# A hybrid decoder block: order of the first weight tile, a cast in two halves, and the spread of the row scale

## Chip, cores and metric

The kernel runs on one core of a Trainium2 chip. The metric is the device time of one execution in microseconds (us), as a median over runs; lower is better.

## What is computed

One decoder layer on 512 tokens of 1024 channels, all in float32. Cut to what matters here:

```python
h = rms_norm(x, g_mix_pre)                  # x * rsqrt(mean(x^2) + eps) * g
z = h @ w_in                                # 1024 x 4608: u_pool | u_rx | u_rg | two gates
xc = causal_dwconv(u_rx, conv_w, conv_b)    # 4 taps along the tokens, 1024 channels
gates = einsum('bshi,ghij->gbshj', xc by 16 heads of 64, w_gates) + b_gates
r, i = sigmoid(gates[0]), sigmoid(gates[1])
log_a = -8 * r * softplus(-lru_lambda)
h_t = exp(log_a) * h_{t-1} + sqrt(-expm1(2 log_a)) * i * xc
y_rnn = (h * gelu(u_rg)) @ w_rg_out
# pooling mixer, gated merge, w_o; then a convolutional FFN and a gated embedding: untouched here
```

## The kernel before

**Arithmetic.** Every large product is made from float32 numbers split in two parts of the type that the trace names fp32r: `hi` is the value cast (on ACT, ScalarE), `lo` is the rest (a subtraction on DVE, VectorE). A product is then three matmuls, hi·hi, hi·lo and lo·hi (`mm3`, L220 to L224). The weight is the loaded operand, the 512 tokens stream past it, so a full matmul is 128 x 128 weights against 512 columns.

**Weights.** `prep(key)` (L450 to L492) issues the transfer of a weight tile into `raw` (on SP's queue), the cast `hi` (ACT, L480; the first tile by pieces, L477) and the subtraction `lo` (DVE, L191 by `sub`). There are six buffers each for raw, hi and lo; the cast of a tile six places later in the list therefore waits until PE (TensorE) has finished with the buffer that it overwrites. `weight(key, ahead)` starts the tiles that come next.

**First stage.** x comes transposed in eight tiles; `ht(k)` is the k-th tile times the gain (hi on ACT L561, lo on DVE L562). The first four channel tiles of u_rx are computed with k outermost (L585 to L591): for each of the eight k, three products times four banks, 96 matmuls. One weight tile, key `("rx", j)`, holds 512 columns for k = 2j and 512 for k = 2j + 1. The scale rsqrt(mean(x²)) of each token is not yet known then; it goes in afterwards, when the banks are read. It is computed as a column per token tile (`rstd1`, 128 x 4, POOL), made into four diagonal matrices (`diag`, DVE L596), and spread over all partitions by four float32 matmuls against a matrix of ones (`spread_rstd`, PE L642), which stand inside the first ordinary channel tile, after its third k. ACT copies the bank to `rb` (L643).

**The recurrent branch's first half.** `in_tile(n)` (L646) is then one channel tile of z at a time, 24 matmuls. Tile by tile around them go: `evac` (DVE L656, times rb, frees the bank), `conv_first` (ACT L674), `conv_rest` (three steps on DVE L680, then the ACT cast L685 of the result), `conv_low` (DVE L689), and, from the sixth tile on, after every second one, `gates` for two channel tiles (PE L700, 12 matmuls with half the rows, six for each tile, alternating between the two banks that each tile has), the eight sigmoids that read these banks (ACT L166) and `gated` (DVE L712). A bank of `gates` is free again when its two sigmoids have read it. In between, DVE computes `decay_columns` (L617 to L636), the softplus of lru_lambda: some twenty operations on tiles of 128 x 8 named `sp`, each needing the one before, with an exponential and a logarithm on ACT; the logarithm needs another function table (ACT_TABLE_LOAD).

**PSUM.** Eight banks rotate. `gates((4, 5))` gives channel tile 5 two banks that `gates((2, 3))` used before it: the second bank of channel tile 2 and the first of channel tile 3. Likewise the first bank of channel tile 1 in `gates((0, 1))` becomes the second bank of channel tile 3 in `gates((2, 3))`.

**Order.** PE's order is the order of the program text. On ACT and DVE a scheduler places the instructions by readiness and priority; `urgent()` and `tc.high_priority` raise it, `behind(a, b)` puts a behind b on the same engine. Each engine then works through its list in that order and waits at the head of it.

Of the kernel before, what the change touches and what calls it, by code (L numbers as in the profile page):

```python
# [9 lines left out]
F32 = mybir.dt.float32  # L10
F32R = mybir.dt.float32r
AF = mybir.ActivationFunctionType
ALU = mybir.AluOpType

P = 128
S = 512
D = 1024
KD = D // P
DFF = 3 * D
NJ = DFF // P  # L20
NT = S // P
# [62 lines left out]
def block_kernel(  # L84
# [21 lines left out]
    ACT, V, PE = nc.scalar, nc.vector, nc.tensor  # L106

    const = ctx.enter_context(tc.tile_pool(name="const", bufs=1))
# [11 lines left out]
    def urgent():  # L120
        return tc.high_priority(offset=URGENT)
# [3 lines left out]
    def nm(s):  # L125
        uid[0] += 1
        return f"{s}{uid[0]}"

    def bank():
        return psum.tile([P, S], F32, tag="ps", name=nm("ps"))  # L130

    def temp(dt=F32, n=S):
        return tmp.tile([P, n], dt, tag="t", name=nm("t"))

    def slot(dt=F32):
        return mid.tile([P, S], dt, tag="m", name=nm("m"))
# [10 lines left out]
    def parts_of(n):  # L147

        return [wpool.tile([P, D], F32R, tag=t, name=nm(t))[:, :n] for t in ("hi", "lo")]

    def tiny(n=1, dt=F32):
        return small.tile([P, n], dt, tag="s", name=nm("s"))

    def behind(ins, name):
        tc.add_manual_dep(
            ins.ins,
            name,
            mybir.DependencyInfo(mybir.DependencyClass.NoSync, mybir.DependencyReason.DATA),
            reason="order on the engine",
        )  # L160
# [29 lines left out]
    def sub(o, a, b):  # L190
        return V.tensor_tensor(o, a, b, ALU.subtract)  # L191
# [7 lines left out]
    def turns(a):  # L199

        return a.rearrange("p (a b) -> p b a", a=2)
# [28 lines left out]
    ident = const.tile([P, P], F32, tag="ident", name="ident")  # L230
    make_identity(nc, ident)
    ones = slot()[:, :P]
# [122 lines left out]
        for kp in range(4):  # L355
            plan(("wpg", kp, h), rows2(w_ple_gate, kp, h))

    ready, low_of, copy_of = {}, {}, {}
    nxt = [0]


# [25 lines left out]
    def up_form(p, f):  # L387

        b = blocks
        if p == 0:  # L390
            t = block(0, f)
        elif p in UP_SUMS:
            t = block(p, {1: 11, 2: 21, 3: 22}.get(f, f))
        elif f == 1:
            for k in (11, 12, 22, 21):
                b[p, k] = block(p, k)
            b[p, 0] = wpool.tile([P, 2, S], F32, tag="sum", name=nm("sum"), bufs=1)
            t = b[p, 11]
        elif f == 6:
            add(b[p, 0], b[p, 11], b[p, 12])  # L400
            t = b[p, 11]
            add(t, b[p, 0], b[p, 22])
        elif f == 7:
            t = b[p, 12]
            add(t, t, b[p, 22])
        elif f == 4:
            t = b[p, 21]
            add(t, b[p, 11], t)
        else:
            t = b[p, {2: 21, 3: 22, 5: 0}[f]]  # L410
        if p == 0 and f != PLAIN[0]:
            late.append((f, t))
            return
        hi, lo = (v.rearrange("p (j c) -> p j c", j=2) for v in parts_of(D))
        if (p, f) in ((1, 1), (1, 5), (1, 7)):
            ins = ACT.copy(hi, t)
            if f != 1:
                behind(ins, h2_done[0])
            later[f] = hi, lo, t
            ready["up", p, f] = (hi, lo)  # L420
            return
        split(hi, lo, t)
        if p == 1 and f != 1:
            behind(last_copy[0], h2_done[0])
        if (p, f) == (1, 4):
            behind(last_sub[0], hid_done[0])
        if p > 2 and f == 6:
            behind(last_copy[0], z_done[0])
        if p > 1 and f == 3:
            behind(last_copy[0], z6_done[p])  # L430
        if p > 1 and f == 7:
            behind(last_copy[0], z_done[0])
        ready["up", p, f] = (hi, lo)
# [16 lines left out]
    def prep(key):  # L450
        if key[0] == "up" and key not in parts:
            up_form(*key[1:])
            return
        if key in parts:
            hi, lo = parts_of(D)
            for i, v in enumerate((hi, lo)):
                nc.sync.dma_start(v.bitcast(F32), parts[key][i])
            if key[0] == "up":
                hi, lo = (v.rearrange("p (j c) -> p j c", j=2) for v in (hi, lo))
            ready[key] = (hi, lo)  # L460
            return
        ap = src[key]
        n = 1
        for d in ap.shape[1:]:
            n *= d
        raw = wpool.tile([P, n], F32, tag="raw", name=nm("raw"), bufs=6)
        dst = raw if len(ap.shape) == 2 else raw.rearrange("p (k c) -> p k c", k=ap.shape[1])
        if key == order[0]:
            nc.sync.dma_start(xraw[0], x_t[0])
            for a, b in FIRST:  # L470
                nc.sync.dma_start(raw[:, a:b], ap.rearrange("p k c -> p (k c)")[:, a:b])
        else:
            nc.sync.dma_start(dst, ap)
        hi, lo = parts_of(n)
        if key == order[0]:
            for a, b in FIRST:
                ACT.copy(hi[:, a:b], raw[:, a:b])  # L477
                sub(lo[:, a:b], raw[:, a:b], hi[:, a:b].bitcast(F32))
        else:
            ins = ACT.copy(hi, raw)  # L480
            last = ins.ins.name
            if key[0] == "wpg" and key[2] == 1:
                behind(ins, last_copy[0].ins.name)
            with tc.high_priority(offset=2 * URGENT if key[0] == "wpg" and key[2] == 0 else 300 if key[0] == "in" and key[1] >= 12 else 0):
                ins = sub(lo, raw, hi.bitcast(F32))
                low_of[key] = ins.ins.name
                copy_of[key] = last
            if key[0] == "wpg" and key[2] == 1:
                behind(ins, last_low[0])
        if key[0] == "rg":  # L490
            hi, lo = (v.rearrange("p (j c) -> p j c", j=2) for v in (hi, lo))
        ready[key] = (hi, lo)  # L492

    def weight(key, ahead=AHEAD):
        i = order.index(key)
        while nxt[0] <= min(i + ahead, len(order) - 1):
            prep(order[nxt[0]])
            nxt[0] += 1
        return ready[key]
# [38 lines left out]
    def ht(k):  # L538
        return hth[k // 4][:, k % 4, :], htl[k // 4][:, k % 4, :]
# [3 lines left out]
    ht_done = []  # L543

    def load_tokens(a):
        xt = quad("C", F32)
        nc.sync.dma_start(
            xt.rearrange("p (a h) c -> p a (h c)", a=2),
            x[2 * a * P : 2 * (a + 1) * P, :].rearrange("(a p) c -> p a c", p=P),
        )  # L550
        xtok.append(xt)

    for k in range(KD):
        raw = xraw[k]
        if k == 0:
            weight(("rx", 0), ahead=0)
        else:
            nc.sync.dma_start(raw, x_t[k])
        hi, lo = ht(k)
        g = gmix[:, k : k + 1]  # L560
        ht_done.append(ACT.activation(hi, raw, AF.Identity, scale=g).ins.name)  # L561
        V.scalar_tensor_tensor(lo, raw, g, hi.bitcast(F32), ALU.mult, ALU.subtract)  # L562
        if k == 3:
            nc.sync.dma_start(col, cols)
        if k % 2 == 1 and k < 7:
            weight(("rx", k // 2 + 1), ahead=0)
        if k in (5, 7):
            load_tokens(k // 2 - 2)
# [4 lines left out]
    for a in range(2):  # L573
        xt = xtok[a]
        for b in range(2):
            v = xt[:, 2 * b : 2 * b + 2, :]
            t = 2 * a + b
# [3 lines left out]
    rstd1 = rsqrt(v4, NT)  # L581
    last_sum[0] = last_pow[0]
    sum_in_dram(chain_of(sums_of("rg"), sums_of("wo"), sums_of("up")), None)
    rx = [bank() for _ in range(4)]
    for k in range(KD):  # L585
        w = weight(("rx", k // 2), ahead=3)
        (wh, wl), (hh, hl) = w, ht(k)
        for i, (a, b) in enumerate(((wh, hh), (wl, hh), (wh, hl))):
            for m in range(4):
                o = (k % 2) * S + m * P  # L590
                PE.matmul(rx[m], a[:, o : o + P], turns(b), start=k == 0 and i == 0, stop=k == KD - 1 and i == 2)  # L591


    diag = temp()
    for t in range(NT):
        behind(V.tensor_scalar(diag[:, t * P : (t + 1) * P], ident, rstd1[:, t : t + 1], None, ALU.mult), low_of["in", 0])  # L596

    bd = quad("C").rearrange("p (s a) c -> p s (a c)", s=2)
    raw = wpool.tile([P, D], F32, tag="raw", name=nm("raw"), bufs=6)
# [38 lines left out]
    def spread_rstd():  # L638
        with urgent():
            ps = bank()  # L640
            for t in range(NT):
                PE.matmul(ps[:, t * P : (t + 1) * P], ones, diag[:, t * P : (t + 1) * P], start=True, stop=True)  # L642
            ina(ACT.copy(rb, ps))  # L643


# [350 lines left out]
    for p in range(2):  # L996
# [8 lines left out]
        if p == 0:  # L1005
            pled = dram.tile([S, D], F32, name="pled")
            pq = []
            for k in range(2):
                raw = temp()
# [232 lines left out]
    d = {}  # L1242
# [212 lines left out]
    for h in range(2):  # L1455
        for t in range(NT):
            i = 2 * (t % 2) + h
            o = temp()
            v = ple[t // 2][:, i, :]
            ins = V.scalar_tensor_tensor(v, v, rp[t], gp[:, h, :], ALU.mult, ALU.mult)  # L1460
# [3 lines left out]
            for a, b in parts:  # L1464
                ps = bank()
# [90 lines left out]
```

## Time and profile before

| what | us |
|---|---|
| three runs | 700.49, 699.56, 700.41 |
| median | 700.41 |
| the profiled execution | 699.78 |
| its span, first to last instruction | 698.0 |
| PE busy in it | 692.4 |
| DVE, ACT, POOL busy in it | 591.4, 453.9, 97.1 |
| granted TensorE clock, mean (1 is full) | 0.998 |

The span is what the instructions cover; 1.8 us of the execution lie outside it. Times inside a trace count from the start of the span. In rows of the timeline the first number is the start in us, the second the time to the end of the group, "x4" the number of instructions in it, and the bracket how long the engine was idle before it and what ended the idle time. PEld is PE's loading of weights, which overlaps its matmuls; a row with a "q" behind the engine's name is its sequencer issuing a transfer. The end of a matmul is modelled, so the pace of PE is read from start to start.

### The profile page before, as it was taken

The page shows a single profiled execution, that of the slowest core. Times are in us where ns is not written, and L with a number is a line of the kernel's source. Part 1 is how long each engine was busy: PE and PEld are TensorE (multiplying, and loading weights), DVE is VectorE, ACT ScalarE, POOL GpSimd, SP SyncE. Part 2 cuts the span into 40 slices and gives each one's busy share as a digit, 9 for nine tenths or more (in the row PEclk, how much of TensorE's full clock was granted, in tenths as well). Part 3 has the DMA queues.
Part 4 walks back from the last instruction along what each step waited for, and adds up shares of the span by engine and source line. Part 5 has one row for each costly group of instructions (what it writes and reads, how often), then busy time and mean ns, then how long its engine had stood idle before and what let it go on. Part 6 is the DMA issues. An engine that isn't in the chain of part 4 may idle for free.

```text
span 698.0 us, 11598 instructions
## 1 busy us (share of the span) xinstructions
PE 692.4 (99%) x4423; PEld 638.1 (91%) x4423; DVE 591.4 (85%) x772; ACT 453.9 (65%) x693; POOL 97.1 (14%) x123
## 2 busy tenths in 40 slices
PE   9999999999999999999999999999999999999997
PEld 8888888888888998899999999999999888888886
DVE  5698735999759998888999999999999989889962
ACT  5857789934447565489966666776667747665631
POOL 0311231321100000112011211210210310001100
PEclk9999999999999999999999999999999999999999
DMA  8999999999998897956387896897799799968011
GB/s 318 408 310 258 251 246 245 264 229 288 261 335 293 301 386 255 346 211 208 115 312 229 191 271 205 202 260 243 173 215 384 241 299 329 343 211 283 29 61 61
DMA packets 67287, 175.71 MB, mean 252 GB/s; under 512 B 6048, under 2 KB 6688, under 8 KB 66848
## 3 DMA queue, kind: packets, MB, share of 16 engines
q1 hardware_dynamic: 49808, 124.64, 49.9%
q0 software_dynamic: 17280, 50.34, 31.0%
q8 instruction: 35, 0.57, 0.3%
q14 instruction: 20, 0.16, 0.1%
q10 hardware_dynamic: 144, 0.00, 0.0%
HBM read 162.37 MB, written 62.91 MB: 323 GB/s over the span
## 4 chain that ended last, share of the span: by engine, by line
PE 99%; DVE 0%; ACT 0%; issue 0%
PE ps L222 31%; PE ps L223 31%; PE ps L224 31%; PE ps L591 3%; PE ps L1034 1%; PE ps L700 1%; PE ps L241 1%; PE ps L642 0%; ACT t L166 0%; DVE t L1474 0%; DVE t L1475 0%; PE ps L1160 0%; DVE m L233 0%; DVE mhalf L235 0%
## 5 line engine op out<-in xcount | busy, mean ns | idle before, releaser
L191 DVE TENSOR_TENSOR lo<-raw,hi 128x1024 fp32r<-128x1024 f32 (+2 forms) x199 | 230.3, 1183 | 46.1 <-ACT hi L480 29.6
L222 PE MATMUL ps<-A,hi 128*128 128x256 f32 (+1 forms) x672 | 211.9, 315 | 0.0
L224 PE MATMUL ps<-A,lo 128*128 128x256 f32 (+1 forms) x672 | 211.4, 315 | 0.0
L223 PE MATMUL ps<-A,hi 128*128 128x256 f32 (+1 forms) x672 | 211.4, 315 | 0.0
L480 ACT CAST hi<-raw 128x1024 fp32r<-128x1024 f32 (+1 forms) x118 | 118.1, 1012 | 56.7 <-PE ps L224 21.5
L222 PEld LDWEIGHTS ps<-A,hi 128*128 128x128 f32 x672 | 128.2, 191 | 8.0 <-issue 1.0
L224 PEld LDWEIGHTS ps<-A,lo 128*128 128x128 f32 x672 | 128.3, 191 | 6.9
L223 PEld LDWEIGHTS ps<-A,hi 128*128 128x128 f32 x672 | 128.3, 191 | 6.8
L222 PE MATMUL ps<-C,hi 128*128 128x256 f32 x376 | 103.4, 275 | 0.0
L223 PE MATMUL ps<-C,hi 128*128 128x256 f32 x376 | 103.2, 275 | 0.0
L224 PE MATMUL ps<-C,lo 128*128 128x256 f32 x376 | 103.2, 274 | 0.0
L195 ACT CAST hi<-raw 128x1024 fp32r<-128x1024 f32 x75 | 77.8, 1051 | 20.5 <-PE ps L223 12.8
L222 PE MATMUL ps<-hi,A 128*128 128x512 f32 x224 | 85.2, 380 | 0.0
L223 PE MATMUL ps<-lo,A 128*128 128x512 f32 x224 | 84.9, 379 | 0.0
L224 PE MATMUL ps<-hi,A 128*128 128x512 f32 x224 | 84.9, 379 | 0.0
L222 PEld LDWEIGHTS ps<-C,hi 128*128 128x128 f32 x376 | 71.8, 191 | 0.2
L223 PEld LDWEIGHTS ps<-C,hi 128*128 128x128 f32 x376 | 71.8, 191 | 0.1
L224 PEld LDWEIGHTS ps<-C,lo 128*128 128x128 f32 x376 | 71.8, 191 | 0.0
L511 POOL TENSOR_TENSOR s<-s,mhalf 128x1 f32<-128x1 f32 (+1 forms) x21 | 17.4, 829 | 262.6 <-DVE s L528 240.0
L307 POOL DMA_DIRECT2D wdsum<-in_w_down_dram x36 | 33.1, 1055 | 141.3 <-ACT t L1170 62.8
L224 PEld LDWEIGHTS ps<-hi,A 128*128 128x128 f32 x224 | 42.3, 189 | 6.0
L223 PEld LDWEIGHTS ps<-lo,A 128*128 128x128 f32 x224 | 42.4, 189 | 5.9
(206 smaller groups left out, 1072.4 us busy)
## 6 DMA issues: line engine op xcount, KB each, us to landing
raw<-in_w_up_dram SPq DMA_DIRECT2D x46, 512.0 KB, 5.9
wdsum<-in_w_down_dram POOLq DMA_DIRECT2D x36, 512.0 KB, 7.6
raw<-in_w_in_dram SPq DMA_DIRECT2D x32, 512.0 KB, 8.0
raw<-wdsum SPq DMA_DIRECT2D x24, 512.0 KB, 8.2
raw<-in_w_down_dram SPq DMA_DIRECT2D x18, 512.0 KB, 7.3
wosum<-in_w_o_dram POOLq DMA_DIRECT2D x12, 512.0 KB, 8.7
wdsum<-wdsum POOLq DMA_DIRECT2D x12, 512.0 KB, 6.6
raw<-wosum SPq DMA_DIRECT2D x8, 512.0 KB, 6.1
```

Source lines behind the costliest of these rows:

```text
L191: return V.tensor_tensor(o, a, b, ALU.subtract)
L195: last_copy[0] = ACT.copy(hi, src)
L222: PE.matmul(o, ah, bh, start=start, stop=False, **kw)
L223: PE.matmul(o, ah, bl, start=False, stop=False, **kw)
L224: PE.matmul(o, al, bh, start=False, stop=stop, **kw)
L241: PE.matmul(wps[:, :P], ones, ones, start=True, stop=True)
L307: ins = nc.gpsimd.dma_start(o, i, **kw)
L480: ins = ACT.copy(hi, raw)
L511: last_pow[0] = nc.gpsimd.tensor_tensor(y, v, mhalf[:, :n], ALU.pow).ins.name
L591: PE.matmul(rx[m], a[:, o : o + P], turns(b), start=k == 0 and i == 0, stop=k == KD - 1 and i == 2)
L700: PE.matmul(ps, bd[pr, a, o], turns(b[pr]), start=i == 0, stop=i == 2)
L1034: PE.transpose(ps[:, q * P : (q + 1) * P], a[:, q * P : (q + 1) * P], ident)
```

## The change

1. The first weight tile (k = 0): PE does all three products for banks 0 and 1, then all three for banks 2 and 3, so that the first six matmuls touch only the first 256 weight columns. For every even k the order of the products becomes (weight hi, x hi), (weight hi, x lo), (weight lo, x hi); before, and still for odd k, the weight's lo comes second.
2. The second weight tile, `("rx", 1)`: its cast and its subtraction are made in two halves of 512 columns. The first half's cast is put behind `ht(2)`'s operation on ACT, the second's behind `ht(3)`'s.
3. The spread: the four scales of a row are split in hi and lo (two 128 x 4 operations), each is multiplied with the identity into one 128 x 512 tile of type fp32r, and two fp32r matmuls of 512 columns against ones cast to fp32r replace the four float32 ones. The two diagonal operations have raised priority.

```diff
--- before.py
+++ after.py
@@ -355,7 +355,7 @@
         for kp in range(4):
             plan(("wpg", kp, h), rows2(w_ple_gate, kp, h))
 
-    ready, low_of, copy_of = {}, {}, {}
+    ready, low_of, copy_of, second = {}, {}, {}, []
     nxt = [0]
 
 
@@ -476,6 +476,10 @@
             for a, b in FIRST:
                 ACT.copy(hi[:, a:b], raw[:, a:b])
                 sub(lo[:, a:b], raw[:, a:b], hi[:, a:b].bitcast(F32))
+        elif key == ("rx", 1):
+            for a, b in (0, S), (S, 2 * S):
+                second.append(ACT.copy(hi[:, a:b], raw[:, a:b]))
+                sub(lo[:, a:b], raw[:, a:b], hi[:, a:b].bitcast(F32))
         else:
             ins = ACT.copy(hi, raw)
             last = ins.ins.name
@@ -559,6 +563,8 @@
         hi, lo = ht(k)
         g = gmix[:, k : k + 1]
         ht_done.append(ACT.activation(hi, raw, AF.Identity, scale=g).ins.name)
+        if k in (2, 3):
+            behind(second[k - 2], ht_done[-1])
         V.scalar_tensor_tensor(lo, raw, g, hi.bitcast(F32), ALU.mult, ALU.subtract)
         if k == 3:
             nc.sync.dma_start(col, cols)
@@ -585,15 +591,31 @@
     for k in range(KD):
         w = weight(("rx", k // 2), ahead=3)
         (wh, wl), (hh, hl) = w, ht(k)
-        for i, (a, b) in enumerate(((wh, hh), (wl, hh), (wh, hl))):
-            for m in range(4):
-                o = (k % 2) * S + m * P
-                PE.matmul(rx[m], a[:, o : o + P], turns(b), start=k == 0 and i == 0, stop=k == KD - 1 and i == 2)
-
-
-    diag = temp()
-    for t in range(NT):
-        behind(V.tensor_scalar(diag[:, t * P : (t + 1) * P], ident, rstd1[:, t : t + 1], None, ALU.mult), low_of["in", 0])
+        three = ((wh, hh), (wl, hh), (wh, hl)) if k % 2 else ((wh, hh), (wh, hl), (wl, hh))
+        for ms in (range(4),) if k else (range(2), range(2, 4)):
+            for i, (a, b) in enumerate(three):
+                for m in ms:
+                    o = (k % 2) * S + m * P
+                    PE.matmul(rx[m], a[:, o : o + P], turns(b), start=k == 0 and i == 0, stop=k == KD - 1 and i == 2)
+
+
+    ones_r = const.tile([P, P], F32R, tag="ones", name="ones")
+    ACT.copy(ones_r, ones)
+    rh, rl = tiny(NT, F32R), tiny(NT)
+    V.tensor_copy(rh, rstd1)
+    sub(rl, rstd1, rh.bitcast(F32))
+    diag = []
+    for r in (rh.bitcast(F32), rl):
+        d = temp(F32R)
+        with urgent():
+            ins = V.tensor_tensor(
+                d.rearrange("p (t c) -> p t c", t=NT),
+                ident[:, None, :].to_broadcast([P, NT, P]),
+                r[:, :, None].to_broadcast([P, NT, P]),
+                ALU.mult,
+            )
+        behind(ins, low_of["in", 0])
+        diag.append(d)
 
     bd = quad("C").rearrange("p (s a) c -> p s (a c)", s=2)
     raw = wpool.tile([P, D], F32, tag="raw", name=nm("raw"), bufs=6)
@@ -638,8 +660,8 @@
     def spread_rstd():
         with urgent():
             ps = bank()
-            for t in range(NT):
-                PE.matmul(ps[:, t * P : (t + 1) * P], ones, diag[:, t * P : (t + 1) * P], start=True, stop=True)
+            for i, d in enumerate(diag):
+                PE.matmul(ps, ones_r, d, start=i == 0, stop=i == 1)
             ina(ACT.copy(rb, ps))
```

The instructions move at three places. First ACT, at the start: `hi_167` is the cast of tile ("rx", 1), `A` the results of `ht`. Before:

```order
L561 ACTIVATE A_135<-m_140,gmix 128x512
L480 CAST hi_167<-raw_165 128x1024
L561 ACTIVATE A_135<-m_141,gmix 128x512
L561 ACTIVATE A_135<-m_142,gmix 128x512
L480 CAST hi_180<-raw_178 128x1024
L561 ACTIVATE A_136<-m_143,gmix 128x512
```

and with the change:

```order
L565 ACTIVATE A_135<-m_140,gmix 128x512
L565 ACTIVATE A_135<-m_141,gmix 128x512
L481 CAST hi_167<-raw_165 128x512
L565 ACTIVATE A_135<-m_142,gmix 128x512
L481 CAST hi_167<-raw_165 128x512
L484 CAST hi_182<-raw_180 128x1024
```

The cast of ("rx", 1), one instruction ahead of two `ht` operations before, is now two, one behind each of them.

Second ACT, around the logarithm of `decay_columns`: `sp` are its 128 x 8 tiles, `hi` casts of coming weight tiles, `m` and `t` the tiles of the convolution; L685 is the cast of a finished convolution. Before:

```order
L480 CAST hi_652<-raw_650 128x1024
L685 CAST m_490<-m_444 128x512
L166 ACTIVATE sp_395<-sp_394 128x8
L480 CAST hi_722<-raw_720 128x1024
L166 ACT_TABLE_LOAD
L166 ACTIVATE sp_396<-sp_396 128x8
L674 ACTIVATE m_556<-t_440,col 128x512
```

and with the change (L685 is now L707, L674 is L696, L480 is L484):

```order
L484 CAST hi_727<-raw_725 128x1024
L707 CAST m_495<-m_449 128x512
L166 ACTIVATE sp_402<-sp_401 128x8
L166 ACT_TABLE_LOAD
L166 ACTIVATE sp_403<-sp_403 128x8
L696 ACTIVATE m_561<-t_445,col 128x512
```

A weight tile's cast that stood behind the cast of a convolution and the exponential now stands ahead of both, and so ahead of the table load and the logarithm; the casts that follow are moved up by one place in the same way.

Third DVE, at the convolution of channel tile 5 (its three steps are those on `m_640` before and `m_645` with the change); L630 to L636 are `decay_columns`, `lo_777` and `lo_782` the same weight tile's subtraction. Before:

```order
L656 TENSOR_TENSOR C_401<-ps_615,rb 128x512
L631 TENSOR_SCALAR sp_396<-sp_396 128x8
L680 SCALAR_TENSOR_TENSOR m_640<-t_494,col,m_640 128x511
L630 TENSOR_TENSOR sp_396<-sp_396,sp_398 128x8
L680 SCALAR_TENSOR_TENSOR m_640<-t_494,col,m_640 128x510
L631 TENSOR_SCALAR sp_396<-sp_396 128x8
L680 SCALAR_TENSOR_TENSOR m_640<-t_494,col,m_640 128x509
L630 TENSOR_TENSOR sp_396<-sp_396,sp_398 128x8
L191 TENSOR_TENSOR lo_777<-raw_774,hi_776 128x1024
L631 TENSOR_SCALAR sp_396<-sp_396 128x8
L689 TENSOR_TENSOR m_646<-m_598,m_645 128x512
```

and with the change (L680 is now L702, L632 to L636 are L654 to L658):

```order
L702 SCALAR_TENSOR_TENSOR m_603<-t_457,col,m_603 128x509
L654 TENSOR_TENSOR sp_403<-sp_403,sp_404 128x8
L655 TENSOR_SCALAR sp_404<-col 128x8
L656 TENSOR_TENSOR sp_403<-sp_403,sp_404 128x8
L657 TENSOR_SCALAR sp_406<-sp_403 128x8
L658 TENSOR_SCALAR sp_407<-sp_403 128x8
L711 TENSOR_TENSOR m_609<-m_561,m_608 128x512
L678 TENSOR_TENSOR C_408<-ps_620,rb 128x512
L702 SCALAR_TENSOR_TENSOR m_645<-t_499,col,m_645 128x511
L191 TENSOR_TENSOR lo_782<-raw_779,hi_781 128x1024
L702 SCALAR_TENSOR_TENSOR m_645<-t_499,col,m_645 128x510
L702 SCALAR_TENSOR_TENSOR m_645<-t_499,col,m_645 128x509
```

The last five operations of `decay_columns` and the weight tile's subtraction, all of them behind the last step of this convolution before, stand ahead of it now. Farther up, between the convolutions of tiles 2 and 5, the same list has more of the `sp` operations directly behind one another, where before another operation stood between two of them. POOL's and SP's orders are the same; PE's differs only by the points above.

## The prediction

> **What bounds the kernel now.** I read the page first, for the engine that is busy, then its chain of waits, then the waits of that engine alone.
>
> ```profile
> span 698.0 us, 11598 instructions
> ...
> PE 692.4 (99%) x4423; PEld 638.1 (91%) x4423; DVE 591.4 (85%) x772; ACT 453.9 (65%) x693; POOL 97.1 (14%) x123
> ...
> PE 99%; DVE 0%; ACT 0%; issue 0%
> ```
>
> ```profile
> engine line waited for: us in total, times, longest us
> PE ps L241 <- DVE mhalf L235: 1.1, 1, 1.1
> ```
>
> PE is busy for 692.4 of 698.0 us, the chain that ended last is PE for 99%, and by the view of waits PE's matmuls wait once, before the warm-up. So whatever PE gains or loses passes straight to the end, as long as no other engine sets a new wait. The change saves PE some tenths of a microsecond at most; it also reorders ACT and DVE, which feed PE. Both sides have to be priced, and the second through the slack that PE's operands and banks have now.
>
> **The first weight tile.** The timeline of the start:
>
> ```profile
> 4.92 2.01 PE L591 MATMUL ps<-A,hi 128*128 128x512 f32 x4
> ...
> 6.11 0.41 PEld L591 LDWEIGHTS ps<-A,hi 128*128 128x128 f32 x2 [0.71 <-ACT hi L477]
> ...
> 6.77 1.03 PE L591 MATMUL ps<-A,lo 128*128 128x512 f32 x4
> ```
>
> PE begins the stage at 4.92, and its third weight load waits for the second piece of the first cast until 6.11. With the change four more matmuls need only the first piece, so the third can start when the second is through. The four of the first row take from 4.92 to the next group at 6.77; from 6.77 on four end-to-end ones keep a pace of about 0.22. At the slower pace of the first rows (some 0.44) the third could start near 5.9 instead of 6.1. That is 0.2 us at the slow pace, 0.1 to 0.2 gained.
>
> **The second weight tile.** The next two views show what stands around its cast; the transfer is the one from which ht(2) is made.
>
> ```profile
> 9.41 1.04 ACT L480 CAST hi<-raw 128x1024 fp32r<-128x1024 f32 x1 [1.53 <-DMA raw<-in_w_rx_dram]
> ...
> 10.36 1.33 ACT L561 ACTIVATE A<-m,gmix 128x512 fp32r<-128x512 f32 x2
> ...
> 11.13 0.51 PEld L591 LDWEIGHTS ps<-A,hi 128*128 128x128 f32 x3 [0.28 <-ACT A L561]
> ```
>
> ```profile
> 3.55 0.43 SPq L558 DMA_DIRECT2D m<-in_x_t_dram  x1
> ```
>
> ```profile
> m<-in_x_t_dram SPq DMA_DIRECT2D x1, 256.0 KB, 6.5
> ```
>
> Now ACT casts the whole weight tile from 9.41, then makes ht(2) from 10.36, and PE waits 0.28 for it until 11.13. ht(2)'s input is issued at 3.55 and lands 6.5 later, at 10.05. With the change the cast of the first half stands behind ht(2), so ACT idles from 9.41 to 10.05 with its weights at hand, does ht(2) (two take 1.33, so 0.67) to about 10.75, and then half a cast. A cast of 128 x 512 lasts 0.62 (row 42.09 below): 11.37. So k = 2 begins 0.24 later than now. What the first tile gained is lost here, since this wait ends by ACT and not by PE. If the cast were quick (half of 1.04, 0.52), the loss would be 0.14; if ht(2) started late by another 0.1, 0.34. I take 0.24. The subtractions on DVE have two whole product groups of time more than the casts, since the weight's lo now comes last.
>
> **The spread.**
>
> ```profile
> 28.50 0.38 PE L224 MATMUL ps<-A,lo 128*128 128x512 f32 x1
> 28.71 1.05 PE L642 MATMUL ps<-t,m 128*128 128x128 f32 x8
> 29.52 0.46 PE L222 MATMUL ps<-A,hi 128*128 128x512 f32 x1
> 29.82 0.38 PE L223 MATMUL ps<-A,hi 128*128 128x512 f32 x1
> ```
>
> ```profile
> 348.88 0.40 PE L1160 MATMUL ps<-hi 128*128 128x512 f32 x1
> 349.12 0.27 PE L222 MATMUL ps<-C,hi 128*128 128x256 f32 x1
> ```
>
> From the L224 at 28.50 to the L223 at 29.82 lie 1.32 us, of which two ordinary matmuls are 0.43: the spread costs 0.89 (the four products show as eight passes). A 512-column product whose columns lie contiguous, as the new ones do, takes 0.24 (348.88 to 349.12); two cost 0.48. PE gains 0.41, bounds 0.3 (a switch of form as before) and 0.46 (pace 0.216). The two wide diagonal operations and the split of the scales run on DVE well over a microsecond ahead; if they were late, PE would wait there for what they lack, tenths again. After the spread PE is ahead by 0.41 - 0.24 = 0.17.
>
> **The reordered ACT and DVE.** This carries the forecast. ACT around the logarithm:
>
> ```profile
> 42.09 0.62 ACT L685 CAST m<-m 128x512 fp32r<-128x512 f32 x1 [2.58 <-DVE m L680]
> 42.62 0.20 ACT L166 ACTIVATE sp<-sp 128x8 f32<-128x8 f32 x1
> 43.19 1.05 ACT L480 CAST hi<-raw 128x1024 fp32r<-128x1024 f32 x1 [0.36 <-PE ps L223]
> 44.26 1.28 ACT L166 ACT_TABLE_LOAD   x1
> 45.55 0.21 ACT L166 ACTIVATE sp<-sp 128x8 f32<-128x8 f32 x1
> ```
>
> The weight cast at 43.19 waits for PE to leave a buffer. It now comes ahead of the convolution's cast (0.53 from start to start) and the exponential (0.12), which therefore queue behind that wait. With PE 0.17 ahead: 43.02 + 0.95 + 0.53 + 0.12 + 1.29 + 0.24 = 46.15 for the subtraction on DVE that needs the logarithm and stands at 45.80 now (next rows): 0.35 later.
>
> ```profile
> 45.80 0.17 DVE L191 TENSOR_TENSOR sp<-sp,sp 128x8 f32<-128x8 f32 x1 [0.72 <-ACT sp L166]
> ...
> 61.00 0.75 DVE L680 SCALAR_TENSOR_TENSOR m<-t,col,m 128x509 f32<-128x509 f32 x1
> ...
> 61.74 1.22 DVE L191 TENSOR_TENSOR lo<-raw,hi 128x1024 fp32r<-128x1024 f32 x1
> 62.88 0.16 DVE L631 TENSOR_SCALAR sp<-sp 128x8 f32<-128x8 f32 x1
> ...
> 63.55 0.16 DVE L632 TENSOR_TENSOR sp<-sp,sp 128x8 f32<-128x8 f32 x1
> 63.74 0.17 DVE L633 TENSOR_SCALAR sp<-col 128x8 f32<-128x8 f32 x1
> 63.95 0.17 DVE L634 TENSOR_TENSOR sp<-sp,sp 128x8 f32<-128x8 f32 x1
> 64.15 0.17 DVE L635 TENSOR_SCALAR sp<-sp 128x8 f32<-128x8 f32 x1
> 64.23 0.16 DVE L636 TENSOR_SCALAR sp<-sp 128x8 f32<-128x8 f32 x1
> ```
>
> ```profile
> 46.00:61.00 15.00, 15.00 (x75) 12.63 (x74) 15.00 (x37) 7.29 (x10) 0.50 (x1) 1.00 1.04 325
> ```
>
> In the windows view (PE, PEld, DVE, ACT, POOL in this order) DVE is busy for all 15.00 us between that subtraction and the last step of tile 5's convolution at 61.00. So whatever enters this stretch of its list delays that step fully. What enters, from behind it: one weight subtraction, 1.14 (61.74 to 62.88); L632 to L636, three of which need the one before: 0.19 + 0.21 + 0.20 + 0.08 + 0.08 = 0.76; and one more pair of L630 and L631, 2 x 0.08 = 0.16. Besides, seven small operations now stand directly behind the one they need. In these rows such a one comes 0.20 after its predecessor, an independent one (64.15 to 64.23) 0.08: 7 x 0.12 = 0.84. Sum 2.90; it is 2.06 if the bunching costs nothing, and some 3.1 if three more waits of that kind arise. I take 2.90, as these rows show the very operations. With the 0.35, tile 5's last step is 3.25 late.
>
> Who waits: ACT's cast of tile 5 and, behind it on ACT, the table load and all sigmoids; PE needs their banks.
>
> ```profile
> 61.84 0.62 ACT L685 CAST m<-m 128x512 fp32r<-128x512 f32 x1 [1.38 <-DVE sp L630]
> ...
> 67.26 0.69 ACT L166 ACTIVATE t<-ps,bias 64x512 f32<-64x512 f32 x1
> ...
> 71.55 1.04 ACT L480 CAST hi<-raw 128x1024 fp32r<-128x1024 f32 x1
> ...
> 81.05 0.68 ACT L166 ACTIVATE t<-ps,bias 64x512 f32<-64x512 f32 x1
> ```
>
> ```profile
> 71.64 0.60 PE L700 MATMUL ps<-m,C 64*128 64x512 f32 x4
> ```
>
> ```profile
> 83.69 0.60 PE L700 MATMUL ps<-m,C 64*128 64x512 f32 x4
> ```
>
> Tile 3 of the second gates (71.64) needs a bank that the sigmoid at 67.26 leaves at 67.95; 3.25 later is 71.20, and PE arrives at 71.47: just in time. In the next round another 0.45 is added. Two weight subtractions stand ahead of gated(1) there, the second behind the cast at 71.55, so that gated(1) comes 1.4 later than by the shift alone; the second subtraction no longer stands inside tile 7's convolution, which gives back 1.14, and some 0.2 is waiting. The sigmoids of gates((2, 3)) are then 3.7 late. The one at 81.05 leaves tile 5's second bank at 81.73 now, and at 85.43 with the change. PE wants that bank 0.11 after 83.69, at 83.80. Its slack of 2.07 is exceeded by 1.63, and with 0.05 until the release is seen and 0.1 for PE to start again the matmul comes 1.8 late. PE's lead of 0.17 is swallowed, because the end of this wait is set by ACT. All that follows runs 1.8 late: ACT and DVE have by then worked off their lists, and the third round's banks have the same slack with PE now later.
>
> **Sum.** 699.78 + 1.8 = 701.6 for an execution like the profiled one, which is 0.6 under the median of the runs (700.41): 702.2 by that. The three runs spread over 699.56 to 700.49; I say 702.0.
>
> **Rivals.** *First, the other side: the delay stays within the slack.* If bunched small operations cost 0.08, the logarithm is not late and the weight subtraction hides in waits, the sigmoids are under 2.07 late and no wait arises. From there on the edits to PE alone count: -0.17, or -0.75 if also the half casts let k = 2 start when PE is ready. 699.0 to 699.6 for the profiled execution, up to 700.2 at the median; no change that a measurement tells. For it: the numbers are close, 3.7 against 2.07, and 0.35 and 0.84 of it are the least sure. Against it: DVE had no idle time in this stretch, and 2.06 of the 2.90 are plain work that moved.
>
> *Second, the delay is larger.* The weight casts, one place earlier on ACT, wait for PE with convolution casts queued behind them, and DVE's next step waits for these; with each such wait all is later. A further 1.0 makes PE wait at 71.47 already, and 2.8 in all: 702.6 to 703.2. For it: the 0.36 at 43.19 is such a wait. Against: in 46 to 61 ACT was busy only 7.29 of 15 us.
>
> *Third, the clock falls in the wait.* At the start PE's matmuls come 0.44 apart and from 6.55 on 0.22. Were a wait of 1.8 us enough to bring the slow pace back, PE would lose half of the slow stretch: 0.8 if it is as long as the one shown here, 4.92 to 6.55, and 2.5 if three times as long: 702.8 to 704.5. [...] No row here shows a wait of this size.
>
> **Chances.** The forecast 0.62 with its own range 701.0 to 703.0, the first rival 0.23, the second 0.12, the third 0.03. What differs by less than 0.2% (1.4 us) a measurement of this kernel cannot tell from no change: slower means over 701.8. The forecast lies above it in about three of four cases (0.46), with the other two 0.59; faster needs under 699.0, the far end of the first rival, 0.03; the rest, 0.38, is no change. The range for 8 in 10 goes from the first rival to the second, 699.9 to 703.4.
>
> **What would show it.** A PE wait of 1 to 2 us on the ACT sigmoid at the second tile of the third gates, near 83.5 to 85.5; the last convolution step of tile 5 near 64.2 on DVE; the logarithm's subtraction near 46.1; k = 2 near 11.37 with a longer wait; the spread at 0.48. No wait at 83.5 makes the forecast wrong; a wait elsewhere, or more than one, makes its place or size wrong.

## The result and the profile after

| | before | changed |
|---|---|---|
| median of nine runs | 700.41 | 702.74 |
| lowest to highest | 699.56 to 702.03 | 700.84 to 703.75 |
| profiled execution | 699.78 | 702.84 |
| its span | 698.0 | 701.0 |

The ratio of the two is 1.0028, 95% interval 1.0015 to 1.0041: slower by 0.15% to 0.41%. (The ratios in this text come from all the runs and are not the quotients of the medians, here 1.0033.)

The page of the changed kernel has hardly another busy time for PE, but another chain:

```profile
span 701.0 us, 11594 instructions
...
PE 693.6 (99%) x4417; PEld 638.2 (91%) x4417; DVE 593.0 (85%) x773; ACT 454.8 (65%) x695; POOL 97.1 (14%) x123
...
PE 92%; DVE 3%; ACT 2%; issue 1%; DMA 1%; SPq 0%; ACTq 0%
```

The 99% of PE have become 92%. Between 42 and 85 us the chain now runs through ACT and DVE, from a weight cast on ACT that itself waits for PE to the sigmoid that ends PE's wait; 4.6 us at the start are a transfer. The view of PE's waits says where PE is held up:

```profile
PE ps L722 <- ACT t L166: 1.4, 2, 0.9
PE ps L241 <- DVE mhalf L235: 1.1, 1, 1.1
PE ps L599 <- ACT hi L477: 0.2, 1, 0.2
PE ps L599 <- ACT A L565: 0.2, 1, 0.2
```

L722 is the gate product. PE's timeline around it, at the third pair of gates:

```profile
82.05 0.95 PE L722 MATMUL ps<-m,C 64*128 64x512 f32 x6
83.49 0.48 PE L722 MATMUL ps<-m,C 64*128 64x512 f32 x1 [0.49 <-ACT t L166]
84.89 0.91 PE L722 MATMUL ps<-m,C 64*128 64x512 f32 x5 [0.92 <-ACT t L166]
85.73 0.75 PE L222 MATMUL ps<-A,hi 128*128 128x512 f32 x1
86.28 0.63 PE L223 MATMUL ps<-A,hi 128*128 128x512 f32 x1
...
88.41 0.63 PE L222 MATMUL ps<-A,hi 128*128 128x512 f32 x1
88.84 0.57 PE L223 MATMUL ps<-A,hi 128*128 128x512 f32 x1
89.25 0.38 PE L224 MATMUL ps<-A,lo 128*128 128x512 f32 x1
```

The same gates before:

```profile
82.94 1.56 PE L700 MATMUL ps<-m,C 64*128 64x512 f32 x12
84.43 0.48 PE L222 MATMUL ps<-A,hi 128*128 128x512 f32 x1
```

Three things stand here. PE comes to these gates at 82.05, 0.89 earlier than before (82.94). It waits there twice, for the sigmoids that free channel tile 5's two banks, and leaves at 85.73, where it left at 84.43 before: it stays 3.68 instead of 1.49, which is 2.19 more, and 1.30 later after the lead of 0.89. And behind the wait its matmuls come 0.43 apart instead of 0.22, until 89.25. The windows view has the clock of this stretch (the column behind POOL; PE's busy time is the first):

```profile
82.00:85.80 3.80, 2.39 (x14) 1.28 (x13) 1.89 (x3) 3.69 (x7) 0.00 (x0) 1.00 1.07 330
85.80:89.30 3.50, 3.50 (x10) 2.80 (x10) 3.03 (x4) 3.44 (x5) 1.54 (x2) 0.51 0.30 123
```

PE is idle for 1.41 of the 3.80 us, and then the granted clock is 0.51 for 3.5 us. The eight steps, from start to start, from 85.73 to 89.25 take 3.52; at the pace of before (0.32 from 84.43 to 84.75, and 26 steps of 0.216 from there to 90.36) they take 0.32 + 7 x 0.216 = 1.83. So 1.69 are lost to the clock, and 1.30 to the wait less PE's lead: 2.99, which is the difference of the spans, 3.0.

### The profile page after: what moved, and what is told of

It reads as the page before. It is cut to its first block, busy times and chain, and to the rows that moved or that the text cites. A ratio compares the mean times of both kernels' runs of the same rounds, so it can differ in the third digit from the quotient of the medians.

```text
span 701.0 us, 11594 instructions
## 1 busy us (share of the span) xinstructions
PE 693.6 (99%) x4417; PEld 638.2 (91%) x4417; DVE 593.0 (85%) x773; ACT 454.8 (65%) x695; POOL 97.1 (14%) x123
## 4 chain that ended last, share of the span: by engine, by line
PE 92%; DVE 3%; ACT 2%; issue 1%; DMA 1%; SPq 0%; ACTq 0%
PE ps L222 29%; PE ps L223 29%; PE ps L224 29%; PE ps L599 3%; DVE m L702 1%; PE ps L1056 1%; DVE lo L191 1%; ACT t L166 1%; DMA m<-in_x_t_dram 1%; ACT m L166 0%; ACT m L707 0%; PE ps L722 0%; DVE m L711 0%; ACT L166 0%; SPq L471 0%
## 5 line engine op out<-in xcount | busy, mean ns | idle before, releaser
L484 ACT CAST hi<-raw 128x1024 fp32r<-128x1024 f32 (+1 forms) x117 | 117.1, 1012 | 66.5 <-PE ps L223 23.4
L224 PEld LDWEIGHTS ps<-hi,A 128*128 128x128 f32 x224 | 42.3, 189 | 6.0
L222 PEld LDWEIGHTS ps<-hi,A 128*128 128x128 f32 x224 | 42.3, 189 | 5.9
```

Source lines behind the costliest of these rows:

```text
L222: PE.matmul(o, ah, bh, start=start, stop=False, **kw)
L224: PE.matmul(o, al, bh, start=False, stop=stop, **kw)
```

## The experiments

**Which part does it.** The theory: the lists of ACT and DVE, which the scheduler reorders, make the sigmoids late. The rival: the start, whose half cast stands behind a late transfer. The first run undoes part 3, the spread:

```diff
-    ones_r = const.tile([P, P], F32R, tag="ones", name="ones")
...
+    diag = temp()
+    for t in range(NT):
+        behind(V.tensor_scalar(diag[:, t * P : (t + 1) * P], ident, rstd1[:, t : t + 1], None, ALU.mult), low_of["in", 0])
...
-                PE.matmul(ps, ones_r, d, start=i == 0, stop=i == 1)
+                PE.matmul(ps[:, t * P : (t + 1) * P], ones, diag[:, t * P : (t + 1) * P], start=True, stop=True)
```

> The change without its third part: the first tile's order and the halved cast stay, the spread is the old one with four float32 products. The lists of ACT and DVE behind the start are then those of before. Theory (the reordered lists make PE wait at the third gates): no PE wait near 83, so between 0.2 slower and 0.6 faster than before, 699.8 to 700.6. Rival (the start itself, the late half cast, costs the time): 702 or more.

Measured 699.94 against 699.99, ratio 0.9993 (0.9982 to 1.0004). PE waits for nothing behind the warm-up in its profile. So the start does not cost the time, and brings nothing that shows.

The second run is its counterpart, the old start with the new spread:

```diff
-        three = ((wh, hh), (wl, hh), (wh, hl)) if k % 2 else ((wh, hh), (wh, hl), (wl, hh))
-        for ms in (range(4),) if k else (range(2), range(2, 4)):
...
+        for i, (a, b) in enumerate(((wh, hh), (wl, hh), (wh, hl))):
...
-        elif key == ("rx", 1):
...
-        if k in (2, 3):
-            behind(second[k - 2], ht_done[-1])
```

> The kernel before with the third part alone: two fp32r products for the spread. The lists of ACT and DVE are reordered as with the whole change. Theory: PE gains 0.4 at the spread and then waits for the sigmoids at the third gates, 1 to 2 in all, with or without a fall of the clock after it: 701.5 to 703. Rival (the start is to blame): 700.0, 0.4 faster.

Measured 702.43 against 699.99, ratio 1.0030 (1.0016 to 1.0043). At the gates its waits are those of the whole change, and its profile has the low clock behind them too, 0.59 over 4.1 us:

```profile
PE ps L714 <- ACT t L166: 1.4, 2, 0.9
...
85.90:90.00 4.10, 4.10 (x13) 3.30 (x13) 3.56 (x4) 4.01 (x6) 2.59 (x4) 0.59 0.38 66
```

So all of it comes with part 3. But part 3 is both a shorter spread and a new order of everything behind it. The next two runs part the two. In order_kept all three parts stay, and four instructions are put back in their old places: the casts of weight tiles 9 to 11 behind the first convolution steps of channel tiles 4 to 6, and the subtraction of weight tile 11 behind the last step of tile 5's.

```diff
@@ prep
+            if key in place:
+                behind(ins, place[key])
...
+            if key[0] == "in" and ("low", key[1]) in place:
+                behind(ins, place["low", key[1]])
@@ conv_first
+        if 3 < c < 7:
+            place["in", 5 + c] = last_func[0]
@@ conv_rest
+        if c == 5:
+            place["low", 11] = last_v[0]
```

> The whole change, with three weight casts put behind the first steps of the convolutions of tiles 4, 5 and 6 and one weight subtraction behind the last step of tile 5's convolution, as they stood before. Theory: no PE wait at the third gates, the clock stays full, and the 0.4 of the spread and what the start gives remain: 699.4 to 700.0, 0.4 to 1.0 faster than before. Rival (the order on ACT and DVE is not what costs): as the changed kernel, 702 to 703.

Measured 699.60 against 699.99, ratio 0.9988 (0.9975 to 1.0000). The scheduler, with these four held, also put the five last small operations back. DVE around the last step of tile 5's convolution, at 61.01 again (L708 is the convolution, L658 to L662 the small operations):

```profile
61.01 0.75 DVE L708 SCALAR_TENSOR_TENSOR m<-t,col,m 128x509 f32<-128x509 f32 x1
61.68 0.16 DVE L656 TENSOR_TENSOR sp<-sp,sp 128x8 f32<-128x8 f32 x1
61.75 1.22 DVE L191 TENSOR_TENSOR lo<-raw,hi 128x1024 fp32r<-128x1024 f32 x1
...
63.56 0.16 DVE L658 TENSOR_TENSOR sp<-sp,sp 128x8 f32<-128x8 f32 x1
```

PE's wait at the gates is gone; a wait of 0.4 for DVE appears late, at 601.6, which the profile of order_kept_again, the same kernel, does not have.

The fourth run takes away only the raised priority of the two diagonal operations, which brings back the old order of ACT and DVE from the convolutions on, but for one small operation on DVE:

```diff
-        with urgent():
-            ins = V.tensor_tensor(
+        ins = V.tensor_tensor(
```

> The whole change without the raised priority of the two wide diagonal operations. The lists of ACT and DVE from the convolutions on are then those of before; the second diagonal stands behind the third weight subtraction on DVE. Theory: no wait at the third gates; a wait of 0.7 to 0.9 for the second diagonal at the spread, which eats what spread and start gain: 700.2 to 700.8. Rival (the order is not what costs): 702 to 703, plus that wait.

Measured 700.70, ratio 1.0006 (0.9992 to 1.0019). No wait at the gates; the second diagonal is late, as expected:

```profile
28.94 0.40 PE L663 MATMUL ps<-t,ones 128*128 128x512 f32 x1
30.28 0.50 PE L663 MATMUL ps<-t,ones 128*128 128x512 f32 x1 [0.94 <-DVE t L610]
```

So the raised priority of two operations of 0.6 us at 26 us is what reordered the lists up to 85 us, and the order is what costs.

**Lateness alone.** The kernel before, with nothing of the change, and DVE made late at the same place; the copies are added work that changes no value:

```diff
@@ conv_rest
         for d in (1, 2, 3):
+            for _ in range(3 if c == 5 and d == 3 else 0):
+                inv(V.tensor_copy(xs[c], xs[c]))
```

> The kernel before, with nothing of the change, and three copies of a 128 x 512 tile onto itself on DVE ahead of the last step of channel tile 5's convolution; the small operations and the weight subtraction that follow it slip ahead of it as in the changed kernel. The step is then 3 to 4 late. Theory (lateness of DVE there is all that costs): PE waits for the sigmoids at the third gates, 1.1 to 2.2, and in executions where the clock falls 1.5 more: 701.2 to 703.5. Rival (it takes the new spread or the new start as well): 700.0 to 700.4.

Measured 701.06 against 699.58, ratio 1.0012 (1.0002 to 1.0022). The time by itself does not decide: the rival's 700.0 to 700.4 would be ratios of 1.0006 to 1.0012, inside this interval. The profile decides. With neither the new spread nor the new start, PE waits at the third gates for the sigmoids, as the theory says:

```profile
63.32 0.75 DVE L682 SCALAR_TENSOR_TENSOR m<-t,col,m 128x509 f32<-128x509 f32 x1
...
PE ps L702 <- ACT t L166: 0.5, 1, 0.5
```

So the rival is out, but the size was off: the wait is 0.5 instead of 1.1 to 2.2, since the step, at 63.32, was only 2.3 late. A copy takes 0.34 to 0.47, and three of the five last small operations stayed behind the step. Of the 1.3 by which the profiled span is longer than before (699.3), 0.65 is there when PE leaves these gates (85.08 against 84.43); a wait of 0.4 for DVE at 602.8 is another part.

**The clock.** After_again is the changed kernel unaltered. In pe_filled, PE repeats gate products in the place of the wait:

```diff
@@ gates
-            for i, (a, b) in enumerate(((0, hi), (0, lo), (1, hi))):
+            for i, (a, b) in [*enumerate(((0, hi), (0, lo), (1, hi)))] * (4 if c == 4 else 1):
```

> The changed kernel unaltered, beside the next three on the same chip. 702.4 to 703; its profile shows either both, the two waits at the third gates and the half pace after them (span about 701), or the waits alone (span about 699.5).

> The changed kernel with the six gate products of channel tile 4 issued four times instead of once (each time from the start of the sum, so the same result). That is 18 more small matmuls, 1.9 us of PE work, in the place where PE waits about 1.9 us for the sigmoids. Theory (PE being idle there brings the clock down for some 3.3 us, at a cost of 1.5 to 1.8): next to no wait, full clock behind it, and 701.0 to 701.6, faster than the changed kernel by 1.0 to 1.7 although PE does more. Rival (the clock falls for another reason, or the half pace is no cost of the wait): as the changed kernel or up to 0.3 slower, 702.4 to 703.

Measured 701.46 (six runs) and 702.28 (five), against 699.58: ratios 1.0030 (1.0019 to 1.0042) and 1.0038 (1.0026 to 1.0050). Both miss what was expected: after_again lies under its 702.4 to 703, pe_filled above the 701.0 to 701.6 of its theory. The profile of after_again has the same two waits and no fall behind them:

```profile
81.80 0.95 PE L722 MATMUL ps<-m,C 64*128 64x512 f32 x6
83.24 0.48 PE L722 MATMUL ps<-m,C 64*128 64x512 f32 x1 [0.49 <-ACT t L166]
84.64 0.91 PE L722 MATMUL ps<-m,C 64*128 64x512 f32 x5 [0.92 <-ACT t L166]
85.49 0.48 PE L222 MATMUL ps<-A,hi 128*128 128x512 f32 x1
85.81 0.38 PE L223 MATMUL ps<-A,hi 128*128 128x512 f32 x1
```

```profile
81.50:85.30 3.80, 2.39 (x14) 1.21 (x12) 1.89 (x3) 3.70 (x6) 0.00 (x0) 1.00 1.09 305
85.30:88.80 3.50, 3.50 (x18) 2.94 (x16) 2.77 (x4) 3.42 (x5) 1.06 (x1) 1.00 0.31 125
```

PE is busy for 2.39 of 3.80 us in both executions, and the clock behind it is 0.51 in the one and 1.00 in the other. The span is 699.0, near the 699.5 expected for the waits alone. In pe_filled PE is busy from 82.30 to 85.98, as long as wait and products take in after_again (81.80 to 85.49), with no wait and no fall:

```profile
82.30 3.75 PE L722 MATMUL ps<-m,C 64*128 64x512 f32 x30
85.98 0.48 PE L222 MATMUL ps<-A,hi 128*128 128x512 f32 x1
86.30 0.38 PE L223 MATMUL ps<-A,hi 128*128 128x512 f32 x1
```

But it was not faster by 1.0 to 1.7, as the theory had it: on this chip only one of the six executions of after_again, at 703.93, had a mean clock as low as 0.997, so there was little to win, and five runs between 701.41 and 703.13 do not tell it from after_again. Two of the five, 702.00 and 703.13, have a mean clock of 1.0, so something else spreads these times as well; what it is stays open. That run decides nothing. The next two make the wait long, in the kernel before, with 16 copies in channel tile 7's convolution; stall_filled adds 15 single products:

```diff
@@ conv_rest, both
+            for _ in range(16 if c == 7 and d == 3 else 0):
+                inv(V.tensor_copy(xs[c], xs[c]))
@@ gates, stall_filled only
+            three = [*enumerate(((0, hi), (0, lo), (1, hi)))]
+            for i, (a, b) in three * 5 if c == 4 else ():
+                PE.matmul(pss[c][0], bd[HEADS[0], a, o], turns(b[HEADS[0]]), start=i == 0, stop=i == 2)
```

> The kernel before, with 16 copies of a 128 x 512 tile onto itself on DVE (0.35 each in the run dve_late, 5.6 in all) ahead of the last step of channel tile 7's convolution. The sigmoids of the second gates are then some 5.6 late, and PE, with 2.1 of slack, idles for 3 to 3.5 at the third gates. Theory (such idleness brings the clock down for some 3.3 us): the profile shows matmuls 0.43 apart behind the wait in every execution, 1.5 to 1.8 lost on top of the wait: 704.2 to 705.5. Rival (the half pace seen before is no cost of a wait): the wait alone, 702.7 to 703.5.

> As stall_long, and PE does the three products of the first bank of channel tile 4 five times more in that place, 15 matmuls, some 3.2 us, each time from the start of the sum, so that it is busy for most of the wait. Theory: no fall of the clock behind it, so 1.3 to 1.8 faster than stall_long although PE does more, 702.7 to 703.7. Rival: the same as stall_long or slower.

Measured 707.71 (707.31 to 707.97, four runs) and 706.42 (705.27 to 707.96, six), against 699.93: ratios 1.0109 (1.0096 to 1.0122) and 1.0088 (1.0073 to 1.0103). In stall_long:

```profile
83.27 0.48 PE L702 MATMUL ps<-m,C 64*128 64x512 f32 x1
86.83 2.19 PE L702 MATMUL ps<-m,C 64*128 64x512 f32 x6 [3.08 <-ACT t L166]
89.63 1.65 PE L702 MATMUL ps<-m,C 64*128 64x512 f32 x5 [0.61 <-ACT t L166]
```

```profile
83.00:86.50 3.50, 0.74 (x3) 0.18 (x1) 3.34 (x5) 1.71 (x3) 0.00 (x0) 0.96 0.95 331
86.50:90.00 3.50, 2.56 (x8) 1.49 (x10) 1.79 (x3) 3.40 (x6) 3.03 (x4) 0.50 0.83 193
90.00:94.00 4.00, 4.00 (x14) 2.81 (x13) 1.57 (x4) 3.88 (x7) 0.51 (x1) 0.62 1.09 187
```

The clock falls, and in every one of the four executions (mean clock 0.994 to 0.995). The time is 2.2 over the upper end expected. PE needs 7.9 from 83.27 to its next product at 91.20, where it needed 1.5 before (82.94 to 84.43): the wait was longer than worked out, and the gate products behind it run at half pace too (the last five take 1.57, 89.63 to 91.20; 0.84 in the changed kernel, 84.89 to 85.73). In stall_filled the long wait is filled, but its second part stays, as two waits of the size of the changed kernel's:

```profile
86.57 0.91 PE L705 MATMUL ps<-m,C 64*128 64x512 f32 x5
87.97 0.48 PE L705 MATMUL ps<-m,C 64*128 64x512 f32 x1 [0.49 <-ACT t L166]
89.38 0.91 PE L705 MATMUL ps<-m,C 64*128 64x512 f32 x5 [0.92 <-ACT t L166]
```

All six executions are above what was expected, which had left these two waits out. They fall in two groups: 705.27, 705.47 and 705.66 at a mean clock of 0.999, and 707.17, 707.39 and 707.96 at 0.996 to 0.997. The profile, in the second group, has the half pace behind this wait:

```profile
90.00:94.00 4.00, 4.00 (x13) 3.04 (x11) 2.42 (x3) 3.89 (x7) 0.90 (x2) 0.57 1.02 165
```

So, as far as the mean clock tells for the executions without a profile, waits of 0.49 and 0.92 let the clock fall in some executions and not in others, and the fall is worth about 1.9. Against stall_long the three without a fall are 2.1 to 2.4 faster although PE does 15 products more, which is the expected sign.

**A version that keeps both.** The new spread alone, with the four instructions held as in order_kept, and order_kept again on another chip:

> The new spread alone, with the same four instructions put back in their old places as in the run order_kept. Theory (first tile and halved cast bring nothing that can be measured): as order_kept, 699.4 to 700.0. Rival (they bring half a microsecond): 700.0 to 700.4.

> The kernel of order_kept unaltered, on another chip, to settle whether it beats the kernel before. Theory: PE is 0.4 to 1.0 ahead behind the start and the spread and waits nowhere up to 600, so 0.9985 to 0.9995 of before. Rival (what PE gains early is lost at a later place where DVE sets the time, as the wait of 0.4 at 601 in the run order_kept): 0.9995 to 1.001.

Spread_kept: 699.65 against 699.58, ratio 1.0011 (0.9998 to 1.0024). Order_kept_again: 699.53 against 700.21, ratio 0.9991 (0.9982 to 1.0000). Twice order_kept came out about 0.1% faster than the kernel before, each time with an interval that just reaches no change; it is the fastest version here: 699.60, where spread_only, with the reordered lists, took 702.43 on the same chip. Whether the first tile and the halved cast have a share in its 0.1% stays open: spread_kept's interval is wide and holds three executions over 702 whose cause was not looked into; of the 23 executions of the kernel before on that chip two are over 702 as well.

## Why the prediction was right, and where not

The time was forecast at 702.0 and came out at 702.74, and the mechanism was the one that was priced: a lateness of DVE, made by the scheduler and not named in the diff, that PE meets at channel tile 5 of the third gates. Point by point, with the rows of the changed kernel:

```profile
9.31 0.72 ACT L565 ACTIVATE A<-m,gmix 128x512 fp32r<-128x512 f32 x1 [1.40 <-DMA m<-in_x_t_dram]
9.94 0.60 ACT L481 CAST hi<-raw 128x512 fp32r<-128x512 f32 x1
...
10.59 0.30 PEld L599 LDWEIGHTS ps<-A,hi 128*128 128x128 f32 x2 [0.18 <-ACT hi L481]
```

- *The first weight tile: not to be told.* k = 1 begins at 7.96 here and at 7.84 in after_again, but at 8.51 in front_only, whose start is the same, and at 8.50 before. The matmuls of the start come 0.43 apart until 6.77 in front_only and until 6.55 before, and 0.22 apart already at 5.2 and 5.5 in the other two. That differs between executions of one kernel by more than the 0.1 to 0.2 that was forecast.
- *The second weight tile: mechanism right, size wrong.* ACT does idle for ht(2)'s transfer, 1.40, with its weights at hand, and PE waits for the half cast. But k = 2 begins at 10.6 and not at 11.37: the transfer landed at 9.3, where the execution before had 10.05. I took one execution's landing for a constant; in front_only ht(2) starts at 9.73. The 0.24 is not to be seen in the time of front_only either.

```profile
28.18 0.63 PE L664 MATMUL ps<-t,ones 128*128 128x512 f32 x2
28.65 0.38 PE L222 MATMUL ps<-A,hi 128*128 128x512 f32 x1
```

- *The spread: right.* 0.47 from 28.18 to 28.65, forecast 0.48.

```profile
42.23 1.05 ACT L484 CAST hi<-raw 128x1024 fp32r<-128x1024 f32 x1 [1.75 <-PE ps L223]
...
45.46 0.17 DVE L191 TENSOR_TENSOR sp<-sp,sp 128x8 f32<-128x8 f32 x1 [0.48 <-ACT sp L166]
```

- *The logarithm: wrong by what PE gained.* The cast that waits for PE starts at 42.23 and not at 43.02, as PE was 0.96 ahead and not 0.17: 0.53 from before the spread (28.18 against 28.71), where a loss of 0.24 was forecast, and 0.43 from the spread. So the subtraction came at 45.46, 0.34 earlier than before instead of 0.35 later.

```profile
62.89 1.52 DVE L702 SCALAR_TENSOR_TENSOR m<-t,col,m 128x510 f32<-128x510 f32 x2
```

- *The stretch on DVE: right.* The second of these two is the last step of tile 5; one takes 0.75, so it starts at 63.66. From 45.46 that is 18.20 against 15.20 before: 3.00 longer, forecast 2.90.

```profile
64.50 0.62 ACT L707 CAST m<-m 128x512 fp32r<-128x512 f32 x1 [3.85 <-DVE m L702]
...
84.15 0.68 ACT L166 ACTIVATE t<-ps,bias 64x512 f32<-64x512 f32 x1
```

- *The sigmoids: right in kind, 0.6 too late.* The cast is 2.66 late (61.84 to 64.50; forecast 3.25), the sigmoids 3.10 (81.05 to 84.15; forecast 3.7). The 0.45 between the two rounds came out at 0.44; what is missing is the logarithm's step.
- *The wait: the place right, mis-sized.* The bank is free at 84.83 (84.15 + 0.68), forecast 85.43, and PE goes on at 84.89. PE is 1.30 behind the kernel before when it leaves the gates, forecast 1.8. The forecast named one wait, and there are two. By its own figures the first was to be expected: 3.7 late, the sigmoid that frees tile 5's first bank ends at 84.02 (80.32 before), and PE wants that bank at 83.69. It costs nothing of its own, since the second ends later. The slack was also read 0.1 too long: the gate products start in pairs, and the first one that needs the second bank stands at 83.70 in the trace before, not at 83.80. The 0.05 for the release and the 0.1 for PE's start were estimates without a row; they came out at 0.06 (84.83 to 84.89) and 0.11 (the five products from there on take 0.84, 84.89 to 85.73, and took 0.73 before, 83.70 to 84.43).
- *PE's lead: the sentence that it is swallowed is wrong.* PE comes to the gates at 82.05, 81.80 and 82.17 in the profiles of the changed kernel, after_again and spread_only, and stays 3.68, 3.69 and 3.68. So what PE gains ahead of 42 us passes through the wait, because the chain that ends the wait begins with a cast on ACT that waits for PE (42.23). The forecast's own sum has this, in the 43.02.
- *The clock: wrong.* The third rival, at 0.03, is what happened in the profiled execution, at 1.69 (priced 0.8 to 2.5). That chance was the author's estimate: no row before had a wait of this size to test it on. Here the clock behind 1.41 us of idleness in 3.80 was 0.51 in the profile of the changed kernel and 1.00 in that of after_again.

So the closeness of the forecast is partly luck: the wait was 0.5 too dear, and the clock, which costs nothing or about 1.7 to 1.9 by the execution, was left out. The run after_again, without the fall, is the case that the sum describes: 700.91 for that execution, forecast 701.6. (The chance for slower, put at 0.59, is 0.61 by its own parts, 0.46 + 0.12 + 0.03.)

## What to carry to other kernels

An operation whose priority is raised can reorder the lists of other engines far behind it: compare the order, not only the diff, and look for instructions that moved ahead of a long in-order chain on a busy engine. A gain on the engine that bounds the kernel has to be set against what the new order costs at that engine's next wait: here PE's lead of 0.89 did pass through, and 2.19 at the gates outweighed it. The wait can cost more than its length, because the clock may fall behind it (here to 0.51 for 3.5 us in one profile, which cost 1.69, and not at all in another of the same kernel); so hold the few instructions that matter in their places before counting the gain. And a landing time read from one execution is a sample, not a constant: ht(2)'s input landed at 10.05 in the profile before and at 9.3 in that of the changed kernel.

## What had not been expected of the hardware

Behind idleness of PE of 0.49 and 0.92 us, the one ending 1.4 before the other, the granted clock was 0.51 for 3.5 us in the profile of the changed kernel and 1.00 in that of after_again, the same kernel; with 3.08 and 0.61, in stall_long, it was 0.50 over 86.5 to 90.0, and all four executions have a mean clock of 0.994 to 0.995. Behind the two short waits the low clock begins 0.9 to 1.6 us after PE's return: at 85.8 against 84.89 in the changed kernel, at 86.6 against 85.01 in spread_only, at 90.5 against 89.38 in stall_filled; in stall_long it begins within the long wait (0.96 over 83.0 to 86.5). Single waits of 0.5 (dve_late, eleven executions) and 0.9 (diag_not_urgent, twelve), each seen in the one profile of its run, left the mean clock at 0.999 or 1.0 in all; by estimate, 3.5 us at 0.51 in a span of some 700 would take about 0.0025 off it. What decides in between was not tried further.
